# Attention scores of a pair of heads: two groups of query tiles instead of four, with two tiles in one PSUM bank

## The chip, the cores and the metric

The kernel runs on one core of a Trainium2 chip. The metric is the device time of one execution in microseconds; the number for a kernel is the median over its runs. The core has five engines with a queue each: TensorE (PE in the profile; its weight loads are PEld), VectorE (DVE), ScalarE (ACT), GpSimd (POOL) and SyncE (SP). Each works through its own instructions in the order of its queue and waits for others by semaphores. TensorE writes its results to PSUM, here eight banks of 128 x 512 float32 values.

## The reference

One layer of a streaming encoder on 512 tokens of width 1024: a half-weighted SwiGLU block, a mixer, a second SwiGLU block, a norm. The mixer has a joint projection into q, k, v (8 heads of 64) and u; attention on q, k, v; a pooling mixer on u; and one output projection.

```python
def hybrid_mixer(h, w_in, q_gain, k_gain, rel_bias, pool_w, pool_scale, w_out):
    proj = h @ w_in
    ...
    a = chunked_attention(q, k, v, q_gain, k_gain, rel_bias)
    p = multiscale_pool(u, pool_w, pool_scale)
    return jnp.concatenate([a, p], axis=-1) @ w_out
```

Within the attention, for each chunk of 64 queries over its own and the eight earlier chunks:

```python
        s = jnp.einsum('bqhd,bkhd->bhqk', qb, kb).astype(jnp.float32) * scale + bias
        valid = (c * CHUNK + kpos - pad) >= 0
        s = jnp.where(valid[None, None], s, NEG_INF)
        p = jax.nn.softmax(s, axis=-1)
        return jnp.einsum('bhqk,bkhd->bqhd', p.astype(vb.dtype), vb)
```

q and k are RMS-normalised per head with learned gains. With 512 tokens the band reaches back to the first token, so a query tile of 128 tokens sees all keys up to its own end.

## The kernel before

Matrices are multiplied in a reduced float32 format. To keep the precision each operand is split into a high and a low part, and a product is three matmuls, high by high, high by low and low by high (`mm3`, lines 176 to 178): 128 x 128 weights against up to 512 columns. Such a triple is called a unit below.

The mixer runs from about 340 to 500 us of the span. Its order on TensorE, VectorE, ScalarE and GpSimd is set by a planner that runs when the program is built. Each piece of work is a generator (a "part") with a rank; `run_parts` (L883) always lets the part of the lowest rank go on that can. A table `clock` holds an estimated time for each engine. `on(engine, cost)` (L873) adds a cost to it, `until(t, engines)` (L898) holds a part back until TensorE's clock has reached t and the engines named are no more than `SLACK` = 2.5 us ahead of it. `take(tag)` (L906) takes a PSUM bank and holds the part until one is free by the clocks; `room` has four banks with the tag "mm" for long products and four with the tag "a" for everything short. When a part issues an instruction, that fixes its place in its engine's queue; at run time semaphores do the waiting. The clocks decide the order alone.

The parts around the change:

- `products()` (L1390), rank 10: the projections in the order q and k of four heads, a part of u, q and k of the other four, v, the rest of u, and then the output projection (`project_out`, L1311). They take what TensorE has free, so they are the filler between all others.
- `scores(pair)` (L1151), rank 0.95 and up: waits for q and k of the pair (the heads 2 pair and 2 pair + 1) and for their bias, and until the head three before has been transposed (`PROBS` = 3 buffers for probabilities). Then, for the query tiles t = 3, 2, 1, 0 in turn, it takes a bank "a" for each of the two heads and issues six matmuls (L1167): three terms of high and low parts by two heads. A head has 64 rows, so head 0 of the pair stands in rows 0 to 63 of TensorE and head 1 in rows 64 to 127. Tile t has (t + 1) x 128 keys: 512, 384, 256, 128. After each tile it gives way to the other parts.
- `softmax(h, t)` (L1128), rank 1.0 + 0.01 h: VectorE adds the bias and takes the row minimum of the negative (L1136), which frees the bank; ScalarE does the exponential with the sum (L1142); VectorE the reciprocal (L1145); ScalarE the normalisation (L1148).
- `head(h)` (L1177): TensorE transposes the probabilities (L1209) in three groups of key tiles, (1, 3), (0), (2): four, four and two transposes. The first group needs the tiles t = 1, 2, 3, the second all four. Each group takes a bank "a"; ScalarE and VectorE copy it out as high and low part (L1188, L1191). Then eight matmuls with v (L1221), and ScalarE (L1231) and VectorE (L1235, L1236) write the head's output and free the bank.
- `pool()` and `pool_map` (L1260, L1292), rank 1.035: window sums of u on GpSimd (L1276) and VectorE, split by ScalarE and VectorE (L131, L132), a unit with the pooling weights `wp` on TensorE into a bank "a", split again with a scale (L134, L135).

ScalarE's and VectorE's queues so hold, in the order in which the planner issued them, softmax steps, copies of transposes, splits of weights (L959, L961, L131, L132) and pool work.

Of the kernel before, what the change touches and what calls it, by code (L numbers as in the profile page):

```python
# [12 lines left out]
ALU = mybir.AluOpType  # L13
# [3 lines left out]
P = 128  # L17
D = 1024
S = 512
# [6 lines left out]
HD = 64  # L26
# [18 lines left out]
ORDER = (0, "u", 1, "v", "u", "u", "u")  # L45
RANK_QK, RANK_HEAD, RANK_POOL, RANK_SCORES = 1.5, 1.0, 1.035, 0.95
HOP = 0.1
SLACK = 2.5
ACT_FIX, DVE_FIX, QK_NORM, NORM = 0.18, 0.08, 2.73, 3.5
AHEAD, NORM_AT, FILL_AT, QK_ROOT = 2, 3, 7, ()  # L50
# [3 lines left out]
def layer(  # L54
# [805 lines left out]
    with tc.tile_pool(name="mix", bufs=1, reuse_waits="tile") as mpool:  # L860
# [12 lines left out]
        def on(engine, cost, *after):  # L873
            clock[engine] = max(clock[engine], *after, clock["pe"] if engine != "pe" else 0.0) + cost
            return clock[engine] + HOP
# [30 lines left out]
        def take(tag):  # L906
            while not room[tag] or min(room[tag]) > clock["pe"]:
                yield min(room[tag]) if room[tag] else None
            room[tag].remove(min(room[tag]))
            return bank(tag, 4)  # L910
# [214 lines left out]

        prob, normal = {}, {}

        def softmax(h, t, sc, f):  # L1128
            n = (t + 1) * P
            yield from until(f, "dve")  # L1130
            p = prob[h, t] = mpool.tile([P, n], F32, tag=f"prob{t}", name=name("prob"), bufs=PROBS)
            nm, tot, rt = (
                small.tile([P, 1], F32, tag=what, name=name(what), bufs=6)
                for what in ("nm", "tot", "rt")
            )
            nc.vector.tensor_tensor_reduce(  # L1136
                p, sc[:, :n], bias[h][0][:, S - n :], -1.0, BIG, op0=ALU.add, op1=ALU.min, accum_out=nm
            )
            f = on("dve", t_dve(n))
            room["a"].append(f)  # L1140
            yield from until(f, "act")
            nc.scalar.activation(p, p, AF.Exp, bias=nm, scale=-1.0, accum_out=tot)  # L1142
            f = on("act", t_act(n) + 0.25)
            yield from until(f, "dve")
            nc.vector.reciprocal(rt, tot)  # L1145
            f = on("dve", 0.16)
            yield from until(f, "act")
            nc.scalar.activation(p, p, AF.Copy, scale=rt)  # L1148
            normal[h, t] = on("act", t_act(n))

        def scores(pair):  # L1151

            heads = (2 * pair, 2 * pair + 1)
            while kT[pair] is None or any(bias[h] is None for h in heads):
                yield None
            while any(h - PROBS >= 0 and h - PROBS not in turned for h in heads):
                yield None
            yield from until(max(kT[pair][1], qT[pair][1], *(bias[h][1] for h in heads)))
            for t in range(NT - 1, -1, -1):
                n = (t + 1) * P  # L1160
                sc = []
                for h in heads:
                    sc.append((yield from take("a")))
                for a, b in ((0, 0), (0, 1), (1, 0)):
                    for i in range(2):
                        rows = slice(i * HD, (i + 1) * HD)
                        nc.tensor.matmul(  # L1167
                            sc[i][:, :n], qT[pair][0][a][rows, t * P : (t + 1) * P],
                            kT[pair][0][b][rows, :n], start=a + b == 0, stop=a == 1,
                        )  # L1170
                f = on("pe", 2 * t_mm3(n))
                for i, h in enumerate(heads):
                    start(softmax(h, t, sc[i], f), RANK_HEAD + 0.01 * h, ("softmax", h))
                yield 0.0
            scored.update(heads)

# [470 lines left out]
```

## Time and profile before

| what | value |
|---|---|
| runs | 867.08, 867.18, 868.5 us, median 867.18 |
| profiled execution, span from its first to its last instruction | 865.4 us |
| score matmuls, L1167 | 96, from 386.8 to 478.7 us |
| transposes of probabilities, L1209 | 80, from 401.0 to 494.5 us |
| products with v, L1221 | 64, from 437.7 to 498.6 us |
| granted TensorE clock, mean of the span | 0.997 |

The span is that of one execution with the profiler; the runs are timed without it, so span and median differ by what lies around the span. In the profile PE is TensorE's matmuls with starts as recorded and modelled ends, so two matmuls that follow each other overlap in their durations; the distance between starts tells what a step costs. A row of the timeline merges instructions of one line that follow each other and gives their count; "idle before" names what ended a wait. The tile names of the program appear without numbers: `mm` and `a` are the PSUM banks, `prob` the probabilities, `pT` their transposes, `m` the split operands, `whi` and `wlo` the high and low part of weights.

### The profile page before, as it was taken

Reading aid. Unit: us, or ns where it says so; the run is one execution under the profiler, and the core shown is the slowest. Engines: PE = TensorE matmul, PEld = TensorE weight load, DVE = VectorE, ACT = ScalarE, POOL = GpSimd, SP = SyncE. Lnnn points to the kernel's source line nnn. Section 1 sums busy time; section 2 is a strip of 40 time slices with the busy share of each in tenths; the row PEclk is TensorE's granted clock in tenths of the full one; section 3 lists DMA queues with packets and bytes.
Section 4 is the critical chain, followed back from the end, with each engine's and each line's share of the span. In section 5 each row is a group of like instructions: output and inputs, shape, how many; then the busy total and the mean of one; then the engine's idle time right before and its main releaser. Section 6 shows DMA issues by size and latency. Waiting matters only on the chain.

```text
span 865.4 us, 14127 instructions
## 1 busy us (share of the span) xinstructions
PE 849.9 (98%) x5296; PEld 755.9 (87%) x5296; DVE 708.1 (82%) x1115; ACT 500.9 (58%) x859; POOL 126.9 (15%) x204
## 2 busy tenths in 40 slices
PE   9999999999999999989999999999999999999996
PEld 7889999999987788867878788889999999988885
DVE  7999888898777868685878676969888898887896
ACT  7445555555556646548656756445555555566573
POOL 0113112211123000120011000102112111122000
PEclk9999999999999999999999999999999999999998
DMA  8168778778899763322212017257778778799832
GB/s 291 59 187 225 214 229 203 187 197 212 244 309 260 239 208 132 113 86 73 80 55 98 25 61 251 78 146 216 217 231 203 188 198 211 246 333 342 273 108 97
DMA packets 72244, 158.50 MB, mean 183 GB/s; under 512 B 6112, under 2 KB 29168, under 8 KB 71792
## 3 DMA queue, kind: packets, MB, share of 16 engines
q1 hardware_dynamic: 49088, 110.93, 36.7%
q0 software_dynamic: 22656, 46.14, 24.9%
q8 instruction: 41, 0.67, 0.3%
q10 hardware_dynamic: 432, 0.54, 0.2%
q14 instruction: 27, 0.22, 0.1%
HBM read 153.38 MB, written 50.34 MB: 235 GB/s over the span
## 4 chain that ended last, share of the span: by engine, by line
PE 89%; DMA 3%; DVE 3%; ACT 2%; issue 1%; SPq 0%; ACTq 0%; DVEq 0%
PE mm L176 21%; PE mm L177 21%; PE mm L178 21%; PE a L177 7%; PE a L178 7%; PE a L176 7%; DMA raw<-wsum 2%; PE a L1167 1%; DMA raw<-in_wB_dram 1%; PE a L1221 1%; PE a L1209 1%; DVE wlo L132 1%; DMA raw<-in_wA_dram 1%; DVE t L1088 1%; ACT prob L1148 1%
## 5 line engine op out<-in xcount | busy, mean ns | idle before, releaser
L132 DVE TENSOR_TENSOR wlo<-raw,whi 128x1024 fp32r<-128x1024 f32 (+2 forms) x115 | 125.3, 1096 | 28.7 <-ACT whi L131 28.4
L131 ACT CAST whi<-raw 128x1024 fp32r<-128x1024 f32 (+2 forms) x115 | 107.3, 944 | 67.8 <-PE mm L177 15.5
L177 PE MATMUL mm<-ha,whi 128*128 128x256 f32 x408 | 115.5, 283 | 0.0
L178 PE MATMUL mm<-ha,wlo 128*128 128x256 f32 x408 | 114.9, 282 | 0.0
L176 PE MATMUL mm<-ha,whi 128*128 128x256 f32 x408 | 114.9, 282 | 0.0
L540 ACT ACTIVATE t<-mm 128x256 f32<-128x256 f32 x102 | 39.3, 386 | 122.5 <-PE mm L178 121.9
L449 DVE TENSOR_TENSOR wlo<-wsum,whi 128x1024 fp32r<-128x1024 f32 x68 | 83.0, 1221 | 14.5 <-ACT whi L444 14.5
L178 PEld LDWEIGHTS mm<-ha,wlo 128*128 128x128 f32 x408 | 77.3, 189 | 0.0
L176 PEld LDWEIGHTS mm<-ha,whi 128*128 128x128 f32 x408 | 77.2, 189 | 0.1
L177 PEld LDWEIGHTS mm<-ha,whi 128*128 128x128 f32 x408 | 77.1, 189 | 0.1
L176 PE MATMUL mm<-hhi,whi 128*128 128x512 f32 x192 | 75.6, 396 | 0.3 <-ACT whi L131 0.2
L177 PE MATMUL mm<-hlo,whi 128*128 128x512 f32 x192 | 75.6, 394 | 0.0
L673 POOL COPY mark<-t 128x1 f32<-128x1 f32 x40 | 14.9, 373 | 409.1 <-DVE t L585 231.1
L178 PE MATMUL mm<-hhi,wlo 128*128 128x512 f32 x192 | 74.8, 391 | 0.0
L675 POOL DMA_DIRECT2D wsum<-in_wB_dram x72 | 70.2, 1086 | 13.2 <-issue 10.1
L444 ACT CAST whi<-wsum 128x1024 fp32r<-128x1024 f32 x68 | 67.9, 1049 | 4.1 <-PE mm L177 3.9
L177 PE MATMUL mm<-wlo,ah 128*128 128x512 f32 x176 | 68.9, 392 | 0.5 <-DVE wlo L132 0.5
L176 PE MATMUL mm<-whi,ah 128*128 128x512 f32 x176 | 68.5, 390 | 0.1
L178 PE MATMUL mm<-whi,ah 128*128 128x512 f32 x176 | 68.5, 389 | 0.0
L449 DVE TENSOR_TENSOR wlo<-raw,whi 128x512 fp32r<-128x512 f32 x68 | 62.3, 952 | 0.3 <-ACT whi L444 0.3
L444 ACT CAST whi<-raw 128x512 fp32r<-128x512 f32 x68 | 56.2, 826 | 8.3 <-PE mm L177 4.4
L177 PE MATMUL a<-wlo,ah 128*128 128x512 f32 (+1 forms) x154 | 55.7, 362 | 1.3 <-DVE wlo L132 1.3
(211 smaller groups left out, 2378.3 us busy)
## 6 DMA issues: line engine op xcount, KB each, us to landing
raw<-in_wA_dram SPq DMA_DIRECT2D x87, 512.0 KB, 5.2
wsum<-in_wB_dram POOLq DMA_DIRECT2D x60, 512.0 KB, 7.2
raw<-wsum SPq DMA_DIRECT2D x40, 512.0 KB, 6.1
raw<-in_wB_dram SPq DMA_DIRECT2D x30, 512.0 KB, 5.7
wsum<-wsum POOLq DMA_DIRECT2D x20, 512.0 KB, 5.4
x<-in_xT_dram SPq DMA_DIRECT2D x16, 256.0 KB, 7.3
raw<-in_wQK_dram SPq DMA_DIRECT2D x8, 512.0 KB, 3.6
raw<-in_wO_dram SPq DMA_DIRECT2D x8, 512.0 KB, 3.4
```

Of the source, the lines that this page charges most:

```text
L131: nc.scalar.copy(hi, src)
L132: nc.vector.tensor_tensor(lo, src, hi.bitcast(F32), op=ALU.subtract)
L176: nc.tensor.matmul(acc, a[0], b[0], start=start, stop=False, **more)
L177: nc.tensor.matmul(acc, a[0], b[1], start=False, stop=False, **more)
L178: nc.tensor.matmul(acc, a[1], b[0], start=False, stop=stop, **more)
L444: nc.scalar.copy(hi, src)
L449: nc.vector.tensor_tensor(lo, src, hi.bitcast(F32), op=ALU.subtract)
L540: nc.scalar.activation(dst, src, AF.Copy, scale=scale)
L673: nc.gpsimd.tensor_copy(mark, after[:, 0:1])
L675: nc.gpsimd.dma_start(self.rows(i, g), self.rows(self.terms[i][at], g), **(dict(accum_op=ALU.add) if at else {}),)
L1088: nc.vector.tensor_tensor(q3, q3, rs[:, t, :].unsqueeze(2).to_broadcast([P, 8, HD]), op=ALU.mult)
L1148: nc.scalar.activation(p, p, AF.Copy, scale=rt)
```

## The change

`scores` goes through the query tiles in two groups, ((3,), (2, 0)) and ((1,),). For the first group it takes four banks "a" before it issues anything, two for tile 3 and two that the tiles 2 and 0 of a head share: 384 + 128 = 512 columns. The 18 matmuls of these three tiles are issued without giving way. The second group takes two banks for tile 1 and issues six matmuls. The softmax parts are started in the order of the tiles 3, 2, 0 and then 1, and a shared bank counts as free when the last tile in it has been read.

The planner's costs change with it: a tile is charged `t_mm3(n)` instead of twice that, and each group is charged `SWITCH` = 0.2 us ahead of it and again behind it.

```diff
+SWITCH = 0.2
...
-        def softmax(h, t, sc, f):
+        def softmax(h, t, sc, f, last):
...
             nc.vector.tensor_tensor_reduce(
-                p, sc[:, :n], bias[h][0][:, S - n :], -1.0, BIG, op0=ALU.add, op1=ALU.min, accum_out=nm
+                p, sc, bias[h][0][:, S - n :], -1.0, BIG, op0=ALU.add, op1=ALU.min, accum_out=nm
             )
             f = on("dve", t_dve(n))
-            room["a"].append(f)
+            if last:
+                room["a"].append(f)
...
-            for t in range(NT - 1, -1, -1):
-                n = (t + 1) * P
+            for group in (((3,), (2, 0)), ((1,),)):
                 sc = []
-                for h in heads:
-                    sc.append((yield from take("a")))
-                for a, b in ((0, 0), (0, 1), (1, 0)):
-                    for i in range(2):
-                        rows = slice(i * HD, (i + 1) * HD)
-                        nc.tensor.matmul(
-                            sc[i][:, :n], qT[pair][0][a][rows, t * P : (t + 1) * P],
-                            kT[pair][0][b][rows, :n], start=a + b == 0, stop=a == 1,
-                        )
-                f = on("pe", 2 * t_mm3(n))
-                for i, h in enumerate(heads):
-                    start(softmax(h, t, sc[i], f), RANK_HEAD + 0.01 * h, ("softmax", h))
+                for _ in group:
+                    sc.append([])
+                    for h in heads:
+                        sc[-1].append((yield from take("a")))
+                on("pe", SWITCH)
+                for ts, banks in zip(group, sc):
+                    at = 0
+                    for t in ts:
+                        n = (t + 1) * P
+                        for a, b in ((0, 0), (0, 1), (1, 0)):
+                            for i in range(2):
+                                rows = slice(i * HD, (i + 1) * HD)
+                                nc.tensor.matmul(
+                                    banks[i][:, at : at + n],
+                                    qT[pair][0][a][rows, t * P : (t + 1) * P],
+                                    kT[pair][0][b][rows, :n], start=a + b == 0, stop=a == 1,
+                                    skip_group_check=True,
+                                )
+                        f = on("pe", t_mm3(n))
+                        at += n
+                    at = 0
+                    for t in ts:
+                        n = (t + 1) * P
+                        for i, h in enumerate(heads):
+                            start(
+                                softmax(h, t, banks[i][:, at : at + n], f, t == ts[-1]),
+                                RANK_HEAD + 0.01 * h, ("softmax", h),
+                            )
+                        at += n
+                on("pe", SWITCH)
                 yield 0.0
```

## The prediction

> **What bounds the kernel now.** I read the page first: the span, and how busy each engine is.
>
> ```profile
> span 865.4 us, 14127 instructions
> PE 849.9 (98%) x5296; PEld 755.9 (87%) x5296; DVE 708.1 (82%) x1115; ACT 500.9 (58%) x859; POOL 126.9 (15%) x204
> ```
>
> TensorE is busy for 849.9 of 865.4 us. Then the stages of the mixer in which the scores stand, by windows (columns: window, its length, busy us and count of PE, PEld, DVE, ACT, POOL, granted clock, DMA share, GB/s).
>
> ```profile
> 386.00:474.00 88.00, 87.89 (x456) 68.95 (x455) 65.54 (x171) 61.18 (x132) 9.14 (x17) 1.00 0.24 79
> 474.00:484.00 10.00, 10.00 (x64) 7.94 (x63) 6.70 (x27) 5.79 (x14) 0.00 (x0) 1.00 0.27 97
> 484.00:491.00 7.00, 5.31 (x31) 4.38 (x30) 4.39 (x11) 6.95 (x21) 0.00 (x0) 1.00 0.00 1
> 491.00:498.00 7.00, 7.00 (x38) 5.78 (x38) 4.66 (x9) 3.22 (x7) 0.00 (x0) 1.00 0.01 2
> ```
>
> From 386 to 484 TensorE has work all the time, so time taken off TensorE counts there. From 484 to 491 the bound is another: ScalarE is busy for 6.95 of 7.00 us and TensorE waits 1.7 us for it. This is the softmax of the last pair of heads. What is saved before has to get past this place.
>
> **The cost of a batch of scores.** The timeline of TensorE around the first pair (columns: start, us, engine, line, operation, tiles, form):
>
> ```profile
> 386.50 0.40 PE L178 MATMUL mm<-whi,hlo 128*128 128x512 f32 x1
> 386.83 0.96 PE L1167 MATMUL a<-m,m 64*128 64x512 f32 x6
> 387.72 0.50 PE L176 MATMUL mm<-whi,hhi 128*128 128x512 f32 x1
> 388.06 0.39 PE L177 MATMUL mm<-wlo,hhi 128*128 128x512 f32 x1
> ...
> 390.93 0.62 PE L1167 MATMUL a<-m,m 64*128 64x256 f32 x6
> ```
>
> The six score matmuls run as three pairs, since each uses 64 of the 128 rows. From the last product before (386.50) to the second one after (388.06) are 1.56 us, for five steps: a product, three pairs, a product. In the last pair of heads two query tiles already stand together:
>
> ```profile
> 474.09 0.39 PE L178 MATMUL mm<-m,wlo 128*128 128x512 f32 x1
> 474.41 1.50 PE L1167 MATMUL a<-m,m 64*128 64x512 f32 x12
> 475.84 0.50 PE L176 MATMUL mm<-m,whi 128*128 128x512 f32 x1
> 476.17 0.39 PE L177 MATMUL mm<-m,whi 128*128 128x512 f32 x1
> 476.40 0.39 PE L178 MATMUL mm<-m,wlo 128*128 128x512 f32 x1
> ```
>
> A step of 512 columns is 0.23 us (476.17 to 476.40). Five of them are 1.15, so a batch costs 1.56 - 1.15 = 0.41 us beside its work. The joined batch takes 2.08 us (474.09 to 476.17) for five steps of 512 and three of 384 (0.17 each): 1.15 + 0.52 = 1.67, and again 0.41 for the batch as a whole. A change of query tile inside a batch is free; going from 128-row products to 64-row scores and back is what costs 0.41.
>
> How many batches there are stands in the order of the two built programs. Before: four for each of the first three pairs, two for the last (512+384, 256+128), 14. After: two for each pair (512+384+128, then 256), 8. Six batches at 0.41 are **2.4 us of TensorE work removed**, all of it ahead of the last pair. Nothing is added: the number of matmuls, reductions, exponentials and DMAs is the same, and the queues of SP and POOL keep their order. What no row shows is the step to a third tile that shares a bank. Its price lies between 0 (the joined batch) and 0.41 (a batch of its own), so at most 4 x 0.41 = 1.6 us; I take 0, since the row is of the same kind.
>
> **What the new order moves.** The planner sees its TensorE clock run faster, and a pair now takes all four banks "a" at once. Up to the last pair's scores the order after has four more units of three products (4 x 0.70 = 2.8 us) and one group of four transposes less (0.4): filler that stood behind these scores now stands ahead of them. So 2.8 - 0.4 - 2.4 = 0 and the last pair starts when it did, but for one wait that goes, because the pool result is now used much later:
>
> ```profile
> PEld mm L177 <- DVE m L135: 0.4, 1, 0.4
> ```
>
> It starts at s = 474.4 - 0.4 = 474.0. **The saving has become filler used up early.** What the end of the mixer then takes is worked out from the rows of ScalarE (ACTIVATE with nm is the exponential, with rt the normalisation):
>
> ```profile
> 476.15 0.72 ACT L1142 ACTIVATE prob<-prob,nm 128x512 f32<-128x512 f32 x1 [3.96 <-DVE nm L1136]
> ...
> 477.90 0.61 ACT L1142 ACTIVATE prob<-prob,nm 128x384 f32<-128x384 f32 x1
> ...
> 482.02 0.69 ACT L134 ACTIVATE m<-a,ps_sb 128x512 fp32r<-128x512 f32 x1 [1.49 <-PE a L178]
> 483.28 0.58 ACT L1231 CAST m<-a 64x512 fp32r<-64x512 f32 x1 [0.57 <-PE a L1221]
> 483.76 0.58 ACT L1188 CAST pT<-a 128x512 fp32r<-128x512 f32 x1
> 484.24 0.62 ACT L1148 ACTIVATE prob<-prob,rt 128x384 f32<-128x384 f32 x1
> 484.76 0.50 ACT L1142 ACTIVATE prob<-prob,nm 128x256 f32<-128x256 f32 x1
> ...
> 485.25 0.39 ACT L1142 ACTIVATE prob<-prob,nm 128x128 f32<-128x128 f32 x1
> ...
> 485.64 0.36 ACT L1188 CAST pT<-a 128x256 fp32r<-128x256 f32 x1
> ...
> 486.40 1.23 ACT L1148 ACTIVATE prob<-prob,rt 128x512 f32<-128x512 f32 x2
> 487.52 0.40 ACT L1142 ACTIVATE prob<-prob,nm 128x128 f32<-128x128 f32 x1
> ...
> 487.90 0.80 ACT L1148 ACTIVATE prob<-prob,rt 128x256 f32<-128x256 f32 x2
> ```
>
> and of TensorE and VectorE:
>
> ```profile
> 481.13 0.39 PE L176 MATMUL a<-m,wp 128*128 128x512 f32 x1
> 481.82 1.43 PE L1221 MATMUL a<-pT,v 128*128 128x512 f32 x8
> 488.46 1.31 PE L1209 MATMUL a<-ident,prob 128*128 128x128 f32 x10 [0.57 <-ACT prob L1148]
> 490.89 0.63 PE L1209 MATMUL a<-ident,prob 128*128 128x128 f32 x4 [1.12 <-DVE m L1236]
> 493.19 1.43 PE L1221 MATMUL a<-pT,v 128*128 128x512 f32 x8
> 497.60 1.44 PE L1221 MATMUL a<-pT,v 128*128 128x512 f32 x8
> ```
>
> ```profile
> 475.41 0.69 DVE L1136 CUSTOM_DVE_ANT_0 prob<-a,bias 128x512 f32<-128x512 f32 x1 [0.42 <-PE a L1167]
> ...
> 489.33 0.68 DVE L1235 TENSOR_TENSOR t<-a,m 64x512 f32<-64x512 f32 x1 [1.13 <-ACT m L1231]
> 490.05 0.69 DVE L1236 TENSOR_TENSOR m<-t,a 64x512 fp32r<-64x512 f32 x1
> ...
> 496.71 1.02 DVE L1191 TENSOR_TENSOR pT<-a,pT 128x512 fp32r<-128x512 f32 x2
> ```
>
> TensorE: the joined batch is 1.43 (474.41 to 475.84) plus three steps of 128 columns, 0.2. Two units of products follow (1.5 with the switch), then the batch of the 256-column tile (0.1 + 0.6), so the last pool product starts at s + 3.8. ScalarE copies it 0.89 later (481.13 to 482.02): s + 4.7. ScalarE's queue is in order, and in the order after this copy (the former L134) stands behind the first two exponentials, which are done by s + 3.1 (VectorE reads 1.0 after the first score, the exponential follows 0.74 later, 0.72 + 0.61). **So ScalarE idles 1.6 us, with the rest of the softmax queued behind it.** From there, by the steps between starts of the rows above: the copy 0.62, exponentials 0.39 + 0.72 + 0.61, the output of head 4 0.48, exponential 0.39, normalisation 0.60, copies of head 5's transposes 0.48 + 0.48 + 0.25, normalisations 0.52 + 0.30, exponential 0.49, normalisations 1.12 + 0.30, exponential 0.49, the output of head 5 0.48, normalisation of the 256-column tile of head 6 0.40: 9.1 us, s + 13.8. The second query tile is now scored last, and the first transposes of head 6 need it; they start some 0.15 later, s + 13.95 = 487.95. Before it was 488.46.
>
> Then ten transposes (0.11 each, 1.1), four of head 7 (0.4; their bank is free at s + 15.0, since head 5's output leaves ScalarE at s + 13.4 and VectorE takes 0.72 + 0.70 and 0.15 to hand over), three units 2.2, four transposes 0.4, one unit 0.8: the product of head 6 with v starts at s + 18.9. From there to head 7's product VectorE's chain decides: before, 493.19 to 496.71 + 0.61, 4.1 us. TensorE has only 1.3 + 0.2 + 1.4 = 2.9 us of work in between (before it had two units more) and waits 1.2. Head 7's product starts at s + 23.1 = 497.1, not 497.60. From there on the two programs have the same order, instruction for instruction.
>
> **Sum.** -2.4 (batches) - 0.4 (the pool wait) + 2.3 (waits in the tail, longer than the 1.7 us of before and without the filler) = -0.5 us, on the profiled execution's 865.4. The runs shown have a median of 867.18, 1.8 above the span, which lies outside it and stays. Forecast: **866.7 us**. A measurement of this kernel tells about 0.2% (1.7 us) from no change, so this counts as no change.
>
> **The rivals.**
>
> *Full saving* (20%). The tail takes no longer than before: 867.18 - 2.8 = 864.4. For it: between 386 and 474 TensorE was busy 87.89 of 88.00 us. Against it: the row of 484 to 491, where ScalarE has no time to give. It would need ScalarE's copy of the pool result out of the way.
>
> *VectorE late behind four banks* (20%), on the other side. A pair holds all four banks until VectorE has read them, in the order tiles 3, 2, 0 of one head, then of the other. Reads start 1.0 after the first score; the 256-column batch needs its second bank at s + 3.2, and the third read ends at about s + 2.6, so 0.5 us is spare. A weight split (one VectorE subtraction over 1024 columns, twice the 0.6 for 512 in the row at 496.71) that stands ahead of the reads can make them 1.2 late, of which TensorE sees 0.7. For it: in the second pair such a split does stand right ahead of the reads. Against: three units of products follow there instead of two. It decides when it strikes three pairs or more, 866.7 + 4 x 0.7 = 869.5 at four.
>
> *The switch is not what is saved* (4%). If the step to the shared bank costs as much as a batch, and half the saving goes, s is 1.6 later: 868.3. The joined batch speaks against it.
>
> *The clock* (3%). The waits before, 0.57 and 1.12 us in the rows above, left the granted clock at 1.00. TensorE's longest wait becomes some 2.3 us (head 5's product ends near s + 11.7, head 6's transposes start at s + 13.95). If that halved the clock for the 4.9 us up to head 6's product, they would take 4.9 us more: 871.6. [...]
>
> **How the numbers follow.** My forecast has 53%, with a range of its own of 865.6 to 867.9: 0.6 for each of the two ends of the tail chain. The range to hold eight in ten reaches to both rivals: **864.4 to 869.4**. Faster by over 0.2% (below 865.4): the full saving and a little of my own case, 23%. Slower (above 868.9): most of VectorE's and the clock's case and unknown waits, 23%. Within: 54%.
>
> **What would show it.** Right: eight batches of scores on TensorE, none with a gap inside; the last pair's first score near 474.0; ScalarE idle for some 1.6 us before the last pool copy; first transposes of head 6 near 488, head 7's product near 497.1; TensorE idle some 4 us between 484 and 498 (before 1.7). Wrong: the last pair starting over 1 us off 474.0, VectorE named as what TensorE's scores or the transposes behind them wait for in several pairs, a granted clock below 1.00, or a tail of ScalarE without the idle time.

## The result, and the profile after

| kernel | median of the runs | profiled execution, span |
|---|---|---|
| before, measured beside it | 867.44 us (867.08 to 869.66) | 865.4 us |
| changed | 871.39 us (869.78 to 872.53) | 870.6 us |

The ratio is 1.0039, with a 95% interval of 1.0029 to 1.0049: the change costs 3.95 us. The forecast was 866.7 and its range ended at 869.4.

The page of the changed kernel, with the windows that were read before and one more (columns as there). Line numbers are each kernel's own: in the changed one the score matmuls are L1175 (before L1167), the transposes L1228 (L1209), the products with v L1240 (L1221), the normalisation L1150 (L1148), the splits L132 and L133 (L131, L132), the pool result's copy L135 (L134) and the reading of a bank of u L1287 (L1268).

```profile
span 870.6 us, 14125 instructions
PE 850.7 (98%) x5296; PEld 759.6 (87%) x5296; DVE 708.5 (81%) x1115; ACT 502.1 (58%) x859; POOL 124.0 (14%) x204
```

```profile
386.00:474.00 88.00, 86.44 (x458) 69.82 (x457) 65.34 (x169) 61.66 (x131) 8.81 (x17) 1.00 0.26 90
474.00:484.00 10.00, 9.70 (x58) 7.45 (x57) 6.52 (x22) 4.34 (x11) 0.00 (x0) 1.00 0.02 7
484.00:491.00 7.00, 5.51 (x30) 4.43 (x30) 4.43 (x17) 6.98 (x21) 0.00 (x0) 1.00 0.01 4
491.00:498.00 7.00, 6.07 (x29) 5.56 (x30) 3.78 (x6) 3.28 (x7) 0.00 (x0) 0.76 0.00 0
498.00:504.00 6.00, 4.72 (x27) 3.83 (x26) 3.48 (x5) 2.27 (x4) 0.00 (x0) 1.00 0.00 0
```

Two things stand out. Between 386 and 474 TensorE now waits 1.56 us where it waited 0.11. And between 491 and 498 it was granted 0.76 of its clock.

To see where the time went, the mixer is cut at four instructions that both kernels have: its first transpose of q and k, the last pair's first score, the product of head 7 with v, and the end. The rows of the timeline of TensorE for the first, before and after:

```profile
379.63 0.38 PE L1096 MATMUL a<-ident,t 128*128 128x128 f32 x2
```

```profile
380.88 0.38 PE L1097 MATMUL a<-ident,t 128*128 128x128 f32 x2
...
477.63 1.78 PE L1175 MATMUL a<-m,m 64*128 64x512 f32 x18
...
502.78 1.43 PE L1240 MATMUL a<-pT,v 128*128 128x512 f32 x8
```

With the rows of before (474.41 and 497.60):

| stretch | before | changed | difference | predicted |
|---|---|---|---|---|
| start to the first q/k transpose | 379.63 | 380.88 | +1.25 | 0 |
| to the last pair's first score | 94.78 | 96.75 | +1.97 | -0.4 |
| to head 7's product with v ("the tail") | 23.19 | 25.15 | +1.96 | -0.1 |
| to the end | 367.80 | 367.82 | 0 | 0 |

The first row is no effect of the change: over the twenty profiles of this study that transpose starts anywhere from 377.43 to 382.40. The two stretches that the change touches give +3.93, within what the runs show (the interval of the ratio is 2.5 to 4.3 us). That it lies 0.02 us from the medians' 3.95 is luck: it holds a fall of the clock that this execution had and that, by their granted clock, not all of the timed ones had (see the last section).

**Ahead of the last pair** the waits stand in the timelines of ScalarE and TensorE:

```profile
466.27 1.14 ACT L132 CAST whi<-raw 128x512 fp32r<-128x512 f32 x2 [0.60 <-DMA raw<-in_wO_dram]
469.60 1.14 ACT L132 CAST whi<-raw 128x512 fp32r<-128x512 f32 x2 [2.19 <-DMA raw<-in_wO_dram]
470.64 0.51 ACT L1150 ACTIVATE prob<-prob,rt 128x256 f32<-128x256 f32 x1
```

```profile
466.59 0.40 PE L177 MATMUL a<-m,wp 128*128 128x512 f32 x1
467.52 0.50 PE L178 MATMUL a<-m,wp 128*128 128x512 f32 x1 [0.53 <-DVE m L133]
...
471.20 1.09 PE L1228 MATMUL a<-ident,prob 128*128 128x128 f32 x8 [0.89 <-ACT prob L1150]
```

ScalarE stands 2.19 us at a piece of output-projection weights (`raw`) that has not landed. Behind it in the queue is a normalisation, and TensorE's transposes wait for that (0.89). A little earlier a pool product comes 0.93 after the one before it, not 0.23, since VectorE is late with its operand. VectorE's queue shows why:

```profile
463.44 0.69 DVE L1287 TENSOR_TENSOR u<-mm,rb 128x512 f32<-128x512 f32 x1
464.05 2.15 DVE L133 TENSOR_TENSOR wlo<-raw,whi 128x512 fp32r<-128x512 f32 x2
466.13 0.74 DVE L136 SCALAR_TENSOR_TENSOR m<-a,ps_sb,m 128x512 fp32r<-128x512 f32 x1
466.79 0.68 DVE L133 TENSOR_TENSOR m<-t,m 128x512 fp32r<-128x512 f32 x1
...
467.46 1.27 DVE L133 TENSOR_TENSOR wlo<-raw,whi 128x512 fp32r<-128x512 f32 x2
```

These operations follow each other without a gap, and ahead of the operand (`m<-t,m`, 466.79) stand the fine parts of a weight piece (464.05, 2.15 us for two).

The same two fine parts set when the late piece is loaded. The load writes into the buffer that they read, so it waits for them (waits of SyncE's queue from 440 to 476 us: in total, times, longest):

```profile
SPq L942 <- DVE wlo L133: 16.9, 4, 8.6
```

They end at 466.20, the load is issued at 466.23 and has landed at 469.58, and ScalarE goes on at 469.60.

**In the tail**, ScalarE and TensorE:

```profile
482.47 0.69 ACT L135 ACTIVATE m<-a,ps_sb 128x512 fp32r<-128x512 f32 x1 [1.69 <-PE a L179]
```

```profile
491.93 3.25 PE L1228 MATMUL a<-ident,prob 128*128 128x128 f32 x14 [2.42 <-ACT prob L1150]
...
502.01 0.47 PE L177 MATMUL a<-m,whi 128*128 128x512 f32 x1 [1.28 <-DVE m L1255]
```

ScalarE idles 1.69 us ahead of the pool copy, and head 6's transposes start 14.3 us after the first score. They are 14 in 3.25 us, where a transpose took 0.11: behind a wait of 2.42 us TensorE ran at half its clock (granted 0.53 from 493.5 to 495.5, see the last section).

### The profile page after: what moved, and what is told of

Read it like the earlier page. It is cut to its first block, busy times and chain, and to the rows that moved or that the text cites. A ratio compares the mean times of both kernels' runs of the same rounds, so it can differ in the third digit from the quotient of the medians.

```text
span 870.6 us, 14125 instructions
## 1 busy us (share of the span) xinstructions
PE 850.7 (98%) x5296; PEld 759.6 (87%) x5296; DVE 708.5 (81%) x1115; ACT 502.1 (58%) x859; POOL 124.0 (14%) x204
## 4 chain that ended last, share of the span: by engine, by line
PE 91%; DVE 3%; DMA 2%; ACT 2%; issue 1%; SPq 0%; ACTq 0%; DVEq 0%
PE mm L177 22%; PE mm L178 21%; PE mm L179 21%; PE a L178 7%; PE a L177 7%; PE a L179 7%; DMA raw<-wsum 1%; PE a L1175 1%; PE a L1228 1%; PE a L1240 1%; DMA raw<-in_wA_dram 1%; DVE wlo L133 1%; DVE t L1089 1%; PE a L1445 0%; PE a L1097 0%
## 5 line engine op out<-in xcount | busy, mean ns | idle before, releaser
L133 DVE TENSOR_TENSOR wlo<-raw,whi 128x1024 fp32r<-128x1024 f32 (+2 forms) x115 | 125.3, 1097 | 29.8 <-ACT whi L132 29.5
L132 ACT CAST whi<-raw 128x1024 fp32r<-128x1024 f32 (+2 forms) x115 | 107.3, 943 | 69.0 <-DMA raw<-in_wB_dram 18.7
```

The source lines that it names most:

```text
L132: nc.scalar.copy(hi, src)
L133: nc.vector.tensor_tensor(lo, src, hi.bitcast(F32), op=ALU.subtract)
```

## The experiments

Eighteen kernels ran, with one profiled execution each. A whole time scatters by 2 us and more from one execution to the next, so each is read first by its profile, in the marks of the table above counted from the first q/k transpose, and then by its ratio to the kernel before in the same comparison. The difference in the fourth column is to before's 117.97.

| run | last pair's first score | tail | head 7's product | difference | ratio (95% interval) |
|---|---|---|---|---|---|
| before | 94.78 | 23.19 | 117.97 | | |
| changed | 96.75 | 25.15 | 121.90 | +3.93 | 1.0039 (1.0029 to 1.0049) |
| reuse | 95.26 | 23.49 | 118.75 | +0.78 | 1.0020 (1.0003 to 1.0037) |
| reuse_before | 94.77 | 23.18 | 117.95 | -0.02 | 1.0008 (0.9995 to 1.0020) |
| warm | 96.75 | 23.51 | 120.26 | +2.29 | 1.0036 (1.0022 to 1.0050) |
| reuse_warm | 95.24 | 23.50 | 118.74 | +0.77 | 1.0020 (1.0007 to 1.0033) |
| supply | 95.28 | 25.01 | 120.29 | +2.32 | 1.0038 (1.0023 to 1.0052) |
| costs_alone | 94.89 | 23.07 | 117.96 | -0.01 | 0.9993 (0.9976 to 1.0009) |
| groups_alone | 98.27 | 20.75 | 119.02 | +1.05 | 1.0014 (1.0001 to 1.0027) |
| pool_behind | 96.83 | 27.22 | 124.05 | +6.08 | 1.0068 (1.0043 to 1.0093) |
| two_first | 94.26 | 24.39 | 118.65 | +0.68 | 1.0014 (1.0003 to 1.0024) |
| two_first_supply | 94.21 | 24.43 | 118.64 | +0.67 | 1.0011 (0.9999 to 1.0023) |
| one_two | 93.20 | 25.92 | 119.12 | +1.15 | 1.0006 (0.9991 to 1.0021) |
| two_first_warm | 94.26 | 25.52 | 119.78 | +1.81 | 1.0015 (1.0001 to 1.0028) |
| light_before | 94.83 | 23.18 | 118.01 | +0.04 | 1.0001 (0.9990 to 1.0012) |
| light_after | 94.22 | 25.10 | 119.32 | +1.35 | 1.0009 (0.9991 to 1.0027) |
| light_two | 92.31 | 24.42 | 116.73 | -1.24 | 0.9988 (0.9973 to 1.0002) |
| gp_two | 93.37 | 24.38 | 117.75 | -0.22 | 0.9996 (0.9986 to 1.0006) |
| gp_after | 96.28 | 23.49 | 119.77 | +1.80 | 1.0030 (1.0019 to 1.0042) |
| gp_before | 94.81 | 23.18 | 117.99 | +0.02 | 1.0000 (0.9988 to 1.0012) |

### Late weights and the clock: reuse, reuse_before, warm, reuse_warm

In reuse two loads of output-projection weights, the fifth and the sixth piece, are left out and the tiles of the two pieces before them are used again; reuse_before does this in the kernel before.

```diff
-            if len(raws) < len(sources):
+            if len(raws) in (20, 21):
+                raws.append(raws[-2])
+            elif len(raws) < len(sources):
```

In warm ten more products of 512 columns (a step of which takes 0.23 us in the rows of before, 476.17 to 476.40), which the transposes then overwrite, stand in the gap ahead of head 6's transposes, so that TensorE is not idle there; reuse_warm has both edits.

```diff
                 tp = yield from take("a")
+                if h == 6 and group == (1, 3):
+                    for _ in range(10):
+                        nc.tensor.matmul(
+                            tp, w_pool[0][:, :P], w_pool[0], start=True, stop=True,
+                            skip_group_check=True,
+                        )
```

> The changed kernel, but the loads of two of the eight pieces of the output projection's weights (the fifth and sixth) are left out and the two pieces before are split again in their place; the order on every compute engine stays the same. Theory A (weights late): ScalarE's queue stood still for 2.8 us because these two pieces had not landed, and this made the last pair's scores 2.0 late; without the loads they start 2.0 to 2.4 us earlier, counted from the first q/k transposes, and the time is 871.4 - 2.2 = 869.2. Theory B (tail: queue order and clock) alone, or theory C (VectorE reads the shared banks late): the last pair starts no earlier and the time stays at 871.4.

> The kernel before with the same two loads left out. Theory A: its weights had landed in time, so nothing is gained: 867.4 within 0.5. If the loads cost time in themselves (traffic, issue) and not by coming late, this one gains too, by 1 us or more.

> The changed kernel with ten extra matmuls of 512 columns on TensorE, into the bank that the first transposes of head 6 overwrite, just ahead of them: 10 x 0.21 = 2.1 us of work within the wait of 2.4 us. Theory B: the transposes behind the wait ran at half clock (0.214 us each, not 0.107); with TensorE kept busy they run at 0.107 and the granted clock stays at 1.00 there, and the time falls by 14 x 0.107 + 0.3 = 1.8 us to 869.6. If the slow transposes have another cause, they stay at 0.214 and the time stays at 871.4 or rises by what the extra work delays.

> Both edits in one: two loads left out and ten extra matmuls. Theories A and B together: the two losses lie one after the other on the same path, so they add: 871.4 - 2.2 - 1.8 = 867.4, within 0.7 of the forecast of 866.7. If theory C or something else holds part of the loss, at least 1 us more remains.

Without the two loads the last pair starts 1.5 us earlier (95.26 for 96.75), not the 2.0 to 2.4 that were expected, and in the kernel before nothing moves: the late piece costs the changed kernel 1.5 us and before nothing. The wait behind VectorE is still there in reuse (0.5 us, on the same product). With TensorE kept busy the tail is 23.51, 1.64 less, so that much was the clock. But reuse has a tail of 23.49 without the extra products. Its own row:

```profile
488.38 1.75 PE L1230 MATMUL a<-ident,prob 128*128 128x128 f32 x14 [2.43 <-ACT prob L1152]
```

The same wait, 2.43 us, and 14 transposes at 0.11. Whether the clock fell behind this wait differs from execution to execution: by their granted clock it seems to have fallen in 7 of 12 of reuse (see the last section). The times of the four runs lie closer together than their intervals are wide; the profiles decide here.

### The planner or the grouping: supply, costs_alone, groups_alone, pool_behind

supply adds a part to the planner that splits a weight piece only 3.6 us after it was asked for (in the changed kernel a piece of 512 KB landed 3.4 us after its issue at the median):

```diff
+            def supply():
+                while len(ready) < len(sources):
+                    i = len(ready)
+                    while i >= first + len(begun) + AHEAD:
+                        yield None
+                    yield from until(ready[i - RAW][2] + LANDING)
+                    prepare()
+                    fetch()
```

costs_alone is the kernel before with the changed kernel's prices; groups_alone the reverse; pool_behind ranks the pool part of the tail behind the softmax.

```diff
-                f = on("pe", 2 * t_mm3(n))
+                on("pe", SWITCH)
+                f = on("pe", t_mm3(n))
...
+                on("pe", SWITCH)
```

```diff
-SWITCH = 0.2
+SWITCH = 0.0
...
-                        f = on("pe", t_mm3(n))
+                        f = on("pe", 2 * t_mm3(n))
```

```diff
-RANKS = {}
+RANKS = {("pool", 0): 0.1}
```

> The changed kernel, with one rule more in its planner: a piece of output-projection weights is split only when the planner's clock says it was asked for 3.6 us ago; every load and every product stays. Counted from the first q/k transpose. Theory A (ScalarE stands at the head of its queue before a weight piece that has not landed): the 2.2 us wait for raw between the third and fourth pairs' scores is gone, the last pair's scores begin at 95.2 to 95.6 (changed kernel 96.75, with the two loads left out 95.26), and the span falls by 1.2 to 1.5 us beside an equal tail. Rival A2 (the splits only become late elsewhere): the wait moves to the products, which then wait for whi, and the last pair's scores stay at 96.5 or later.

> The kernel before with its four score groups, but the changed kernel's prices in the planner (a score group costs 1 x its price plus two switches of 0.2 in place of 2 x its price). Theory A1 (the cheaper price lets the planner place splits and loads closer together than the loads can land, the grouping has no part): the last pair's scores begin 1 us or more later than in the kernel before (94.78 from the first q/k transpose), and the time is 1 us or more over before's. Rival A3 (the loss needs the joined groups, which shorten the real work as well): the last pair's scores begin within 0.5 of 94.8 and the time is within 0.5 us of before's.

> The changed kernel's joined groups and shared bank with the prices of before in the planner (2 x the price, no switch). By Theory A1 the saving of 2.4 us shows: the last pair's scores begin at 95.2 or earlier, no wait for raw over 1 us between the third and fourth pairs' scores, and the time is 1.5 us or more under the changed kernel's. By Rival A3 the wait for raw stays at 2 us and the last pair's scores begin at 96.5 or later.

> The changed kernel with the pool part ranked behind the softmax of the last pair, so that ScalarE does not stand 1.7 us before the pool copy at its queue's head. Theory B1 (that copy's place lengthens the tail): head 7's product with v begins 22.0 or less after the last pair's first score (changed kernel 25.15, 23.5 without the slow clock). Rival B2 (the clock): with the pool product taken from the gap, TensorE stands still 2.5 us or longer before head 6's transposes, they run at 0.21 us each, and the same stretch stays at 24 or more.

supply starts the last pair at 95.28, as Theory A said, but its clock fell in the tail (25.01), and its time is no better than the changed kernel's. costs_alone stays within 0.12 us of before in every mark of the table: the new prices alone do nothing, and Theory A1 falls. groups_alone has the wait for the weight piece although it pays the old prices:

```profile
ACT whi L132 <- DMA raw<-in_wO_dram: 2.7, 2, 2.3
PE a L1228 <- ACT prob L1150: 1.3, 2, 1.0
PE mm L178 <- DVE m L1255: 0.9, 1, 0.9
PE a L178 <- DVE m L133: 0.5, 1, 0.5
```

(From its waits between 380 and 505 us: who waited for what, us in total, times, longest.) So the joined groups themselves bring the lateness, as Rival A3 has it. Its last pair starts late (98.27), with one more unit of filler ahead of it than in the changed kernel, but TensorE's longest wait in the tail is only 0.9, the clock stays, and head 7's product comes at 119.02. Its ratio is 1.0014. The prices so do nothing with before's groups, but with the joined ones the order that they lead to has the long wait in the tail.

pool_behind refutes B1. ScalarE no longer idles before the pool copy (it now waits 2.28 us for head 4's output instead), and the tail is longer, 27.22. Its timeline of TensorE:

```profile
485.59 0.47 PE L177 MATMUL a<-m,wp 128*128 128x512 f32 x1 [1.11 <-DVE rt L1147]
...
487.04 2.79 PE L1240 MATMUL a<-pT,v 128*128 128x512 f32 x8 [0.52 <-DVE pT L1210]
491.45 0.79 PE L177 MATMUL mm<-m,whi 128*128 128x512 f32 x1 [1.62 <-ACT m L135]
...
497.52 0.49 PE L179 MATMUL mm<-m,wlo 128*128 128x512 f32 x1
```

Eight products with v that took 1.43 take 2.79 here, and the product at 491.45 0.79 where it would take 0.4 to 0.5; the row of 497.52 is the first near its usual length again. The clock fell at about 487.5 (granted 0.92 from 478.0 to 489.3, then 0.50), behind the waits of 1.11 and 0.52; the one of 1.62 came later. So B2 has the right end with the wrong condition: the clock fell here without a wait over 2.5 us.

### Another cut of eight batches: two_first, two_first_supply, one_two, two_first_warm

The joined group takes four banks at once, and the order puts 3.4 us more filler ahead of the last pair than is needed for two. Three other cuts:

```diff
-            for group in (((3,), (2, 0)), ((1,),)):
+            for group in (((3,),), ((2, 0), (1,))):
```

in two_first (also eight batches; with supply's part in two_first_supply, and with warm's products as well in two_first_warm), and in one_two, with twelve batches,

```diff
-            for group in (((3,), (2, 0)), ((1,),)):
+            for group in (((3,),), ((1,),), ((2, 0),)):
```

> The changed kernel with its eight batches cut differently: tile 3 alone in the first (two banks), tiles 2 and 0 in a shared bank and tile 1 in the second (four banks). Theory D (the joined batch waits until all four banks are free, so more other TensorE work is put ahead of it, and the tail behind it has a fixed length): 3.4 us of other products move from ahead of the last pair's first score to behind it, which then begins at 93.3 from the first q/k transpose if the wait for a weight piece stays whole (changed kernel 96.75) and at 91.8 if it goes; with a tail of 23.5 head 7's product begins at 115.3 to 116.8 (kernel before 117.97, changed 121.90), 1.2 to 2.7 us less time than before, 1.65 more if the clock falls. Rival E (the four banks are only asked for later): the second batch waits until tile 3's softmax has read its banks, the tail grows to 25 us or more, and head 7's product begins at 118 or later.

> The same with weight pieces split only when they were asked for 3.6 us ago. Theory A with D: the last pair's first score at 91.8 to 92.3, no wait for raw over 1 us between the third and fourth pairs' scores, head 7's product at 115.3 to 116. Rival E: as above, 118 or later.

> Tile 3, then tile 1, then tiles 2 and 0 in a shared bank, each batch with two banks: 12 batches in place of the 14 before and the 8 of the change. Theory D: 4.1 us of other products move behind the last pair's first score against the changed kernel, and 2 x 0.41 us of switches are saved against before; the first score at 92.3 (plus up to 2.2 for late weights), head 7's product at 115.5 to 118. Rival E: the number of banks of a batch has no part in it, the first score stays at 95 or later and head 7's product at 118.5 or later.

> The eight batches cut as in the first run of this call, weight pieces split late, and ten further products of 0.23 us in the gap ahead of head 6's transposes. Theory B (clock): these transposes run at 0.11 us each and the tail is 23.5 us; if the run without the further products shows 0.21 us, head 7's product comes 1.6 us earlier here. If the further products are more than the gap holds, it comes later by the excess, at most 2.3 us.

Neither theory had this. With 3.4 us of filler less ahead of it the last pair starts only 2.5 us earlier than in the changed kernel, at 94.26, and head 7's product comes at 118.65, later than before. TensorE's waits of two_first between 464 and 472 us, and VectorE's queue ahead of them:

```profile
468.30 0.50 PE L177 MATMUL mm<-m,whi 128*128 128x512 f32 x1 [1.01 <-DVE u L1287]
470.07 0.50 PE L178 MATMUL a<-m,wp 128*128 128x512 f32 x1 [0.57 <-DVE m L133]
```

```profile
463.95 1.62 DVE L1210 TENSOR_TENSOR pT<-a,pT 128x512 fp32r<-128x512 f32 x3
465.49 0.68 DVE L1302 SCALAR_TENSOR_TENSOR t<-us,u 128x512 f32<-128x512 f32 x1
...
466.36 1.29 DVE L133 TENSOR_TENSOR wlo<-raw,whi 128x512 fp32r<-128x512 f32 x2
467.57 0.68 DVE L1287 TENSOR_TENSOR u<-mm,rb 128x512 f32<-128x512 f32 x1
```

TensorE waits for VectorE to read a bank of u (L1287), and VectorE has been busy without a gap since 463.95, again with the fine parts of a weight piece just ahead. In one_two the first score comes at 93.20, but head 6's first transposes now also wait for the larger tile 2, scored last, and the tail grows to 25.92. In two_first_warm the clock had been at full speed without the extra products (1.00 granted in the tail of two_first_supply), and they only cost their 1.1 us. So far every kernel with joined groups whose clock stayed up (a mean of 0.997 or 0.998 in the profiled execution) and that had no extra products (reuse, groups_alone, two_first, two_first_supply, one_two) has head 7's product at 118.6 to 119.1, later than before, however its saving was cut. The tail of two_first, 24.4, has two more waits for VectorE in it (0.90 and 0.85, for the outputs of heads); these were not followed further.

### VectorE relieved: light_before, light_after, light_two

The fine parts of four pieces of output-projection weights are left out, eight VectorE operations of 0.64 us; the products take the coarse part in their place, so TensorE's work stays. The planner's prices stay, and so do the orders of the other engines.

```diff
-                    split(raws[i][:, j * S : (j + 1) * S], hi[j], lo[j])
+                    nc.scalar.copy(hi[j], raws[i][:, j * S : (j + 1) * S])
                     t = on("dve", t_dve(S), on("act", t_act(S)))
-                ready.append((hi, lo, t))
+                ready.append((hi, hi, t))
```

light_before does it in the kernel before, light_after in the changed one, light_two in the cut of two_first.

> The kernel before without the fine parts of four pieces of output-projection weights (the products take the coarse part in their place): eight VectorE operations of 0.64 us fewer, TensorE's work as it was. Theory F (VectorE's queue is what the joined batches run into) has nothing to take away here: last pair's first score at 94.3 to 94.8, head 7's product at 117.4 to 118.0 from the first q/k transpose. Rival G (the softmax chain of the last pair): the same.

> The changed kernel with the same left out. Theory F: the waits for m behind VectorE (0.7) and for the weight piece (the raw buffers come free earlier; 1.1 at TensorE) go, the last pair's first score moves from 96.75 to 94.4 to 95.0, where the prediction had it, and head 7's product begins at 117.5 to 118.5, 1.65 later if the clock falls. Rival G: the first score still at 96 or later, or a tail longer than 24 without the slow clock.

> The other cut of eight batches (tile 3 alone first) with the same left out. Theory F: its waits of 1.0 and 0.6 between the third and fourth pairs' scores go, the first score moves from 94.26 to 92.4 to 92.8, and with a tail of 23.5 to 24.4 head 7's product begins at 116 to 117.2, a microsecond or more ahead of the kernel before with the same left out. Rival G: the tail grows by what the first score gained, and head 7's product stays within 0.5 of the kernel before with the same left out.

Theory F holds. Nothing moves in the kernel before. In the changed kernel the last pair's first score moves by 2.5 us, from 96.75 to 94.22, and TensorE has neither wait any more: the pool operand comes in time, and of ScalarE's wait for the weight piece 0.49 us are left of 2.19, as its buffer is free earlier. In the other cut it moves to 92.31, the tail keeps its 24.4, and head 7's product is 1.28 us ahead of light_before. The changed kernel's tail stayed at 25.10, because here too the clock fell, and at another place:

```profile
487.96 2.23 PE L1228 MATMUL a<-ident,prob 128*128 128x128 f32 x14 [2.43 <-ACT prob L1150]
489.85 0.78 PE L177 MATMUL mm<-m,whi 128*128 128x512 f32 x1
...
492.13 0.57 PE L179 MATMUL mm<-m,whi 128*128 128x512 f32 x1
492.53 0.39 PE L177 MATMUL mm<-m,whi 128*128 128x512 f32 x1
```

### The work kept, on another engine: gp_two, gp_after, gp_before

GpSimd computes those fine parts in place of VectorE; nothing is left out.

```diff
-                    split(raws[i][:, j * S : (j + 1) * S], hi[j], lo[j])
+                    part = raws[i][:, j * S : (j + 1) * S]
+                    nc.scalar.copy(hi[j], part)
+                    nc.gpsimd.tensor_tensor(lo[j], part, hi[j].bitcast(F32), op=ALU.subtract)
```

> The other cut of eight batches, with the fine parts of four pieces of output-projection weights computed on GpSimd in place of VectorE; nothing left out. Theory F: the last pair's first score at 92.3 to 93.0 (94.26 with the splits on VectorE, 92.31 with them left out), head 7's product at 116.7 to 117.5, half a microsecond or more ahead of the kernel before (117.97), and the time 0.5 to 1.3 us under before's. Rival H (GpSimd takes longer for a split than VectorE, 1.2 us or more for 512 columns, and holds up its window sums or the products that need the fine part): new waits for wlo or u behind GpSimd, first score at 94 or later, head 7's product at 118.5 or later.

> The changed kernel with the fine parts on GpSimd. Theory F: last pair's first score at 94.2 to 95.0 (changed kernel 96.75), head 7's product at 117.7 to 118.5, 1.65 later if the clock falls. Rival H: first score at 96 or later.

> The kernel before with the fine parts on GpSimd. Theory F: nothing to gain, first score at 94.8 and head 7's product at 118.0. Rival H: first score at 95.5 or later.

Half of each. In gp_two the last pair starts at 93.37, between 94.26 and 92.31, and the time is before's (0.9996, 0.9986 to 1.0006). From 440 to 500 us, its group of GpSimd (busy us, mean ns of one, idle before and what ended it) and then a wait of TensorE:

```profile
L956 POOL TENSOR_TENSOR wlo<-raw,whi 128x512 fp32r<-128x512 f32 x8 | 10.9, 1388 | 12.6 <-ACT whi L955 6.9 <-PE a L179 5.5
```

```profile
PE mm L179 <- POOL wlo L956: 1.2, 2, 0.9
```

A fine part takes 1388 ns there against some 640 on VectorE (1.27 to 1.29 for two), and TensorE now waits 1.2 us for it: F and H each have a share. In gp_after the weight piece stays late (2.4 us at ScalarE) and the last pair starts at 96.28; gp_before stays with before. No kernel of the study is shown to be faster than before.

## Why the prediction was wrong, step by step

**The batches: right.** There are eight of them, and the joined one is the row of 18 matmuls at 477.63 above. The products around it:

```profile
477.31 0.39 PE L179 MATMUL mm<-m,wlo 128*128 128x512 f32 x1
477.63 1.78 PE L1175 MATMUL a<-m,m 64*128 64x512 f32 x18
479.35 0.50 PE L177 MATMUL mm<-m,whi 128*128 128x512 f32 x1
479.69 0.40 PE L178 MATMUL mm<-m,whi 128*128 128x512 f32 x1
```

From the product before it (477.31) to the second one after it (479.69) are 2.38 us, for five steps of 512 columns (1.15), three of 384 (0.52) and three of 128 (0.2): 0.51 for the whole batch where 0.41 was taken. The third tile in the shared bank costs at most 0.1. The work did leave TensorE.

**"So 2.8 - 0.4 - 2.4 = 0 and the last pair starts when it did, but for one wait that goes": this step failed.** It put the first score 94.4 us after the first q/k transpose; it came at 96.75. The sum treated every microsecond taken off TensorE as a microsecond gained, because TensorE had been busy 87.89 of 88.00 us. That row says who was last, not by how much the others were ahead. With the work squeezed, TensorE asks earlier for what VectorE makes (banks read, pool operands split) and for weight pieces whose buffer VectorE must have read before the next load, and VectorE was not ahead by 2.4 us. light_after shows it: with 5.1 us of VectorE work away the first score comes at 94.22, where the sum had it. Of the 2.5 us, 1.5 went with the late weight piece (reuse); in the changed kernel's rows the pool product shows another 0.7; the rest is not assigned.

The sum also counted the four units of filler that moved ahead of the last pair on TensorE alone. They are products with output-projection weights, and a piece of these came with them: the changed kernel splits four pieces ahead of the last pair's first score, on ScalarE at 459.60, 462.84, 466.27 and 469.60, and the fourth is the late one. The kernel before splits three, and the fourth behind its first score of 474.41:

```profile
476.87 1.13 ACT L131 CAST whi<-raw 128x512 fp32r<-128x512 f32 x2
```

So ScalarE and VectorE each had over a microsecond more to do in that stretch. What this one piece costs by itself was not tried. The rival of VectorE had the engine right and the place wrong: no matmul of scores shows a wait.

**The tail: right but for the clock.** The chain was worked out at 23.1 us from the first score to head 7's product; where the clock stayed up it took 23.5 (reuse, warm, reuse_warm). ScalarE idled 1.69 us where 1.6 was said, head 6's transposes came at 14.3 where 13.95 was said, and TensorE's longest wait was 2.42 where some 2.3 was said. The last step, from head 6's product to head 7's, was put at 4.1 us; it takes 4.4 in both kernels, before too (493.19 to 497.60). And 18.9 + 4.1 is 23.0, not 23.1.

**The clock: its chance was too small.** The wait was foreseen, and a slow clock behind it was given 3%. It fell in the profile of the changed kernel and of three more of its kind, at a price of 1.64 us (25.15 against 23.51), not 4.9: half speed held for 3.4 us (below), not up to head 6's product. The 3% was the author's estimate, and no run shows the 4.9 us of its sum: the clock fell behind one wait of 2.42 or 2.43 us in three kernels, for 3.4 us each, and behind two waits of 1.11 and 0.52 us in a fourth, for 10.2 us with further waits within it. That this rival's time, 871.6, lies beside the measured 871.39 is luck: its 4.9 us were three times the price, and it started from a last pair that came 2.4 us earlier.

**The end: right.** From head 7's product on the two take the same time.

In the terms of the forecast: -2.4 was taken off TensorE; what was forecast at -0.4 by the last pair's start came as +1.97, and the tail, forecast at -0.1, as +1.96, of which 1.64 is the clock. That the saving would not shorten the kernel was said; that the waits behind VectorE would cost another 2.4 us ahead of the last pair was not.

## What to carry to other kernels

An engine that is busy without a gap may have another right behind it: before counting work taken off the first as time, look how long ahead of its use each operand was ready, and repeat the change with that other engine's work left out. Joining small pieces of work also changes when buffers are asked for, so count what is moved ahead of the joined piece, on every engine that it needs, and the buffers it needs at once. Where a change opens a wait on TensorE like the 2.42 us here, price the slow clock behind it (here 1.64 us), and read short differences from marks inside the profile rather than from whole times that scatter by 2 us.

## What the runs showed of the hardware

**The slow clock followed some of these waits and not others, and held for 3.4 us in three profiles and for 10.2 in a fourth.** The same wait of 2.42 or 2.43 us was followed by half speed at once (changed, supply), about a microsecond later (light_after), or not at all (reuse, gp_after). How long it held is estimated from the granted clock, the last figure but two of these windows of the changed kernel and then of light_after:

```profile
491.50:493.50 2.00, 1.57 (x8) 1.57 (x9) 1.25 (x2) 1.20 (x3) 0.00 (x0) 0.61 0.00 0
493.50:495.50 2.00, 2.00 (x10) 1.92 (x9) 1.64 (x3) 1.31 (x4) 0.00 (x0) 0.53 0.00 0
495.50:497.00 1.50, 1.50 (x8) 1.21 (x7) 0.77 (x2) 0.30 (x1) 0.00 (x0) 1.00 0.00 0
```

```profile
487.00:489.00 2.00, 1.03 (x9) 1.04 (x10) 1.38 (x2) 1.63 (x4) 0.00 (x0) 1.00 0.00 0
489.00:491.00 2.00, 2.00 (x10) 1.81 (x9) 1.72 (x4) 1.59 (x4) 0.00 (x0) 0.52 0.00 0
491.00:493.00 2.00, 2.00 (x8) 1.55 (x7) 0.54 (x1) 0.00 (x0) 0.00 (x0) 0.63 0.00 0
```

If the clock is either full or half (0.50 stood from 489.3 to 496.7 in pool_behind), a window of w us with a mean of c holds 2w x (1 - c) us of half speed: 1.56 + 1.88 = 3.4 us in the changed kernel, 1.92 + 1.48 = 3.4 in light_after, from 489.1 to 492.5, and 1.40 + 2.00 + 0.04 = 3.4 in supply (0.65 from 491 to 493, 0.50 up to 495, 0.99 up to 497). In pool_behind, with further waits within it, the slow clock held from 487.5 to 497.7 (0.92 from 478.0 to 489.3, 0.50 up to 496.7, 0.94 up to 505.2): 1.8 + 7.4 + 1.0 = 10.2 us. What decides whether it falls and for how long isn't settled by these runs.

How often it fell in the timed executions can be estimated from the granted clock that each has for its whole length. A fall of 3.4 us takes 1.7 of 870 us off, 0.002. A mean of 0.996 or less stands at 3 of 8 executions of the changed kernel, 7 of 12 of reuse, 10 of 12 of supply, 7 of 12 of light_after and 8 of 12 of gp_after, which all have the long wait, but at none of the 21 of warm and reuse_warm, where TensorE was kept busy through it, and at 9 of 154 of the kernel before. So the slow clock was nearer to an even chance than to 3%. A mean does not say where in an execution the clock fell.

**A pair of VectorE's subtractions took 2.15 us beside a window sum of GpSimd, and 1.27 to 1.29 elsewhere.** In the changed kernel the two fine parts at 464.05 took 2.15 us where its other three pairs take 1.27 to 1.29. In that time GpSimd ran a window sum, which took 1.37 where the two others on `u` after 440 us took 1.06 (the one at 378.11 took 1.37 as well):

```profile
454.25 1.06 POOL L1295 TENSOR_TENSOR us<-u 128x527 f32<-128x527 f32 x1 [0.69 <-DVE rt L1147]
...
464.28 1.37 POOL L1295 TENSOR_TENSOR us<-u 128x527 f32<-128x527 f32 x1 [0.77 <-DVE u L1287]
```

GpSimd's sum ends at 465.65. The first of the two fine parts took 0.68 us; the second started at 464.65 and took 1.55, up to 466.20, where the other six took 0.67 to 0.69. In the kernel before the two fine parts at 465.81 took 2.03 us, its other three pairs 1.28 to 1.29, and a window sum that started at 465.31 took 1.38. Why they were slow beside each other was not tried by itself.
